# Seven products instead of eight for pairs 3 and 6 in the last projection's later blocks

## The chip, the core and the metric

The kernel runs on one core of a Trainium2 chip. Its engines, each with an instruction queue of its own that runs in order, are TensorE (PE, with the weight loads PEld), VectorE (DVE), ScalarE (ACT), GpSimd (POOL) and SyncE (SP). DMAs are issued here by SP and by POOL, a few by ACT, and 16 DMA engines move the data. The metric is the time of one execution on the device in microseconds (us); lower is better. Before the change the median of three runs is 2599.01 us (2597.99 to 2599.30).

## What is computed

Two layers of an encoder over 256 tokens of 4096 features. Each layer normalises, projects with one matrix to 11264 columns, mixes by grouped attention in one half of the features and by a retention in both directions in the other, and projects back with a 4096 x 4096 matrix:

```python
for l in range(DEPTH):                       # 2
    h = rmsnorm(x, norm_w[l])
    proj = h @ w_in[l]                       # 256 x 4096 @ 4096 x 11264
    ...
    x = x + jnp.concatenate([a_out, r_out], axis=-1) @ w_out[l]   # 4096 x 4096
return rmsnorm(x, final_norm)
```

All of it is float32. The change lies in the last product with `w_out` (the second layer's).

## The kernel before

**Stages and blocks.** The four projections are stages 0 to 3; stage 3 is the second layer's output projection. A stage is cut into blocks of 1024 output columns (two halves of 512), and stage 3 has four of them, b = 0 to 3. Within a block the 4096 rows of the weights are taken as 16 pairs of 128-row tiles, p = 0 to 15. A pair is a 2 x 2 block product: two halves of 128 tokens, two row tiles, two column halves, so eight products of 128 x 128 x 512, added up in eight banks M1 to M8 (in the profile all are called M).

**Eight or seven.** Some pairs are done with seven products instead, by a Strassen-like scheme: PE then multiplies sums of operand quarters by sums of weights, and the banks are combined at the block's end (`combine`; `last_combine` in the last block). `SEVENS` lists these pairs: 2, 5, 8, 9, 11 and 13 in every stage. Operands of a seven-product pair have seven forms: three quarters as they are (A11, A12, A22) and four sums (S1 to S4).

**Three matmuls a product.** PE takes float32r parts, so each operand and weight is split into a high part (a cast on ACT) and a low part (the difference, on DVE), and a product is high x high, high x low and low x high. `whi` and `wlo` are the two parts of a weight page, `x8h` and `x8l` those of an eight-product pair's operand, `x7h` and `x7l` those of a seven-product pair's. The first two matmuls are on L1683, the third on L1693. A page is 128 x 1024 numbers (512 KB) and serves several products.

**Weights of a pair.** An eight-product pair has two pages, loaded by SP into one of six buffers `wraw` and split. A seven-product pair loads one `wraw` page (kind A); ACT copies it to `wv`, POOL adds a prepared second tensor to that by an accumulating DMA (`twice_out`, kind T), SP loads half a page `third` (kind B, split into `bhi` and `blo`), and DVE forms `wu` from these three by two additions (kind U). The `twice` tensors are laid out on the host for the pairs of `EVER`, which are all pairs in `SEVENS`.

**What sets the order.** The program is recorded once in Python, and the order of every engine's queue is the order of recording. `block` walks over the products in the order of `GROUPS` (each group starts with a seven-product pair; eight-product pairs behind it are interleaved by `pages_of`); the class `Weights` keeps the pages ahead, with 5 buffers `whi` and 4 `wlo`. A planner with its own clocks for DVE and ACT (`tick`, `room`, `Lane`) slips in other work: output sums, `out_tasks`, operand splits. 13 buffers `pg` (`page`) hold everything else. In the last layer `out_task` loads a page `gain` by SP, and DVE multiplies the block's result by it (`ca<-ca,gain`, `cb<-cb,gain`).

**Operands.** `split_operand` and `split_pair` make a stage's operand parts from rows that `Turn` fetches from `next_dram`, two pairs at a time; the fetched page is dropped when both are split.

**The last block.** `last_combine` adds the residual, loaded by four DMAs of SP into the operand buffers of pairs 0 and 1 as soon as these are used up, and scales the output. The pairs in `DELAYED` (10, 12, 14, 15) leave their last products to the very end; parts of their weight pages are kept in operand buffers of pairs that are done (`dead_room`), so names such as `x7h` then hold weights.

Of the kernel before, what the change touches and what calls it, by code (L numbers as in the profile page):

```python
# [17 lines left out]
P = 128  # L18
# [144 lines left out]
def constants():  # L163
# [48 lines left out]
]  # L212

GROUPS = [
    ([tuple(range(_s[0]))] if _s[0] else []) + [tuple(range(_a, _b)) for _a, _b in zip(_s, _s[1:] + (NP,))] for _s in SEVENS
]
SPREAD = (3, 5, 8, 11, 12, 13)
SPREAD1 = (4, 7, 8, 10, 12, 14)
# [11 lines left out]
    return order  # L230


def grouped(order, stage):

    groups = []
    for p in order:
        if p in SEVENS[stage] or not groups:
# [6 lines left out]
FIRST_GROUPS = [grouped(_o, _i) for _i, _o in enumerate(FIRST_ORDER)]  # L244
# [4 lines left out]
def pages_of(group, stage, first=False):  # L249

    n = 1 if group[0] in SEVENS[stage] else 0
# [12 lines left out]

def slots_of(group, stage, first=False):

    for _p, _k in pages_of(group, stage, first):
        if _p in SEVENS[stage] and not (first and _p in NATIVE):
# [68 lines left out]
def hybrid_encoder(  # L337
# [451 lines left out]
    def split_pair(p, v, whole, stage):  # L789
# [748 lines left out]

    def lead(stage):

        return 8 * SEVENS[stage][0]

    def block(after_pair, phase, then, first_order=False, opening=False, order=LAST_ORDER, last=None, hurried=False):

# [42 lines left out]
        def begin_product(n, name, p, index, k, h):  # L1587
# [508 lines left out]
```

## Time and profile before

| | |
|---|---|
| median of 3 runs | 2599.01 us |
| the profiled execution | 2599.34 us |
| its span, first to last instruction | 2597.6 us |
| granted TensorE clock, mean | 0.998 |
| PE busy | 2581.8 us, 11560 matmuls |
| DVE, ACT, POOL busy | 2215.3, 1853.6, 398.6 us |
| moved by DMA | 653.52 MB, 252 GB/s in the mean |

The page gives each engine's busy time and its share of the span, then groups of equal instructions with their count, busy time, mean length, and the idle time of the engine just ahead of them with what ended it (after the arrow). A timeline row has its start and length in us, the engine, the line, the operation, what it writes and reads, and in brackets the idle time before it. In the table by windows an engine's busy time is followed by its number of instructions, and the last three columns are PE's granted clock, the mean busy share of the DMA engines and GB/s. Nearly all of DVE's and ACT's work is on L321, since a helper records it, so one goes by the names.

### The profile page before, as it was taken

To read this page: it belongs to the slowest core of one execution; us is meant where nothing else is said; L and a number is where in the kernel's file an instruction comes from. 1 tells how busy PE (TensorE), PEld (TensorE's weight loads), DVE (VectorE), ACT (ScalarE), POOL (GpSimd) and SP (SyncE) were. 2 spreads that over 40 slices of the span, in tenths; PEclk is the share of its full clock that TensorE was granted. 3 is DMA by queue.
4 is the path that set the end of the run, shared out by engine and by line. 5 is a ranking of instruction groups with operands and counts; after the bars stand their busy time and mean duration, and the time that the engine had idled before them with its cause. 6 is when DMAs were issued, how large, how long until landed. Compare 5 with 4: busy or idle time off the path is not lost.

```text
span 2597.6 us, 34368 instructions
## 1 busy us (share of the span) xinstructions
PE 2581.8 (99%) x11560; PEld 2135.2 (82%) x11560; DVE 2215.3 (85%) x2710; ACT 1853.6 (71%) x2626; POOL 398.6 (15%) x548
## 2 busy tenths in 40 slices
PE   9999999999999999999999999999999999999998
PEld 7888888888888888888878888888888888888886
DVE  7898888888789898777979888889888798987777
ACT  8877777766666788656887667776666667886655
POOL 0111221221102100211111112221201021000000
PEclk9999999999999999999999999999999999999999
DMA  9988988888778778988888879888887787788886
GB/s 314 305 237 277 289 242 254 281 247 263 221 220 260 230 235 227 271 269 248 275 253 261 250 239 279 246 270 268 259 257 222 208 259 242 220 229 251 250 243 194
DMA packets 206594, 653.52 MB, mean 252 GB/s; under 512 B 24784, under 2 KB 31440, under 8 KB 206416
## 3 DMA queue, kind: packets, MB, share of 16 engines
q1 hardware_dynamic: 147040, 472.99, 51.8%
q0 software_dynamic: 58656, 177.24, 30.7%
q8 instruction: 90, 1.47, 0.2%
q10 hardware_dynamic: 720, 1.10, 0.1%
q14 instruction: 88, 0.72, 0.1%
HBM read 607.19 MB, written 44.04 MB: 251 GB/s over the span
## 4 chain that ended last, share of the span: by engine, by line
PE 94%; DMA 2%; DVE 2%; ACT 1%; issue 1%; SPq 0%; DVEq 0%; POOLq 0%; POOL 0%; ACTq 0%
PE M L1683 60%; PE M L1693 30%; PE M L1158 1%; PE M L1157 1%; PE M L1156 1%; DMA ca<-in_x 1%; DVE wlo L321 1%; ACT whi L321 1%; DMA third<-in_w_out 0%; PE M L1677 0%; DMA wraw<-in_w_out 0%; DVE cb L321 0%; DMA whole<-in_w_in 0%; ACT ca L321 0%; DVE ca L321 0%
## 5 line engine op out<-in xcount | busy, mean ns | idle before, releaser
L321 DVE TENSOR_TENSOR wlo<-wraw,whi 128x1024 fp32r<-128x1024 f32 (+1 forms) x774 | 935.3, 1215 | 172.8 <-issue 61.2
L321 ACT CAST whi<-wraw 128x1024 fp32r<-128x1024 f32 (+1 forms) x776 | 800.1, 1045 | 297.1 <-PE M L1683 283.0
L1683 PE MATMUL M<-whi,x8h 128*128 128x512 f32 x2368 | 922.5, 390 | 1.0 <-DVE cb L321 0.8
L1683 PE MATMUL M<-whi,x8l 128*128 128x512 f32 x2368 | 921.8, 389 | 0.0
L1693 PE MATMUL M<-wlo,x8h 128*128 128x512 f32 x2364 | 676.3, 389 | 0.2 <-DVE wlo L321 0.2
L1683 PEld LDWEIGHTS M<-whi,x8h 128*128 128x128 f32 x2368 | 444.6, 188 | 94.9 <-DVE cb L321 1.5
L1683 PEld LDWEIGHTS M<-whi,x8l 128*128 128x128 f32 x2368 | 444.6, 188 | 92.4 <-DVE x8l L321 0.3
L1693 PEld LDWEIGHTS M<-wlo,x8h 128*128 128x128 f32 x2364 | 442.2, 188 | 91.4 <-DVE wlo L321 1.0
L1683 PE MATMUL M<-whi,x7h 128*128 128x512 f32 x1080 | 420.5, 389 | 0.2 <-ACT whi L321 0.2
L1683 PE MATMUL M<-whi,x7l 128*128 128x512 f32 x1080 | 420.3, 389 | 0.0
L1693 PE MATMUL M<-wlo,x7h 128*128 128x512 f32 x1080 | 334.4, 390 | 0.7 <-DVE wlo L321 0.6
L729 POOL DMA_DIRECT2D wv<-in_twice_in x132 | 118.5, 898 | 1068.6 <-ACT wv L321 923.8
L321 ACT CAST whi<-wu 128x1024 fp32r<-128x1024 f32 x180 | 189.3, 1052 | 91.9 <-DVE wu L321 54.2
L321 ACT CAST whi<-wv 128x1024 fp32r<-128x1024 f32 x180 | 189.0, 1050 | 91.5 <-PE M L1683 51.9
L321 DVE TENSOR_TENSOR wlo<-wv,whi 128x1024 fp32r<-128x1024 f32 x180 | 219.6, 1220 | 37.3 <-PE M L1693 30.7
L321 ACT COPY wv<-wraw 128x1024 f32<-128x1024 f32 x180 | 188.9, 1049 | 74.7 <-DMA wraw<-in_w_out 35.2
L321 DVE TENSOR_TENSOR wlo<-wu,whi 128x1024 fp32r<-128x1024 f32 x180 | 219.1, 1217 | 24.8 <-PE M L1693 16.7
L1693 PEld LDWEIGHTS M<-wlo,x7h 128*128 128x128 f32 x1080 | 202.4, 188 | 44.1 <-DVE wlo L321 2.5
L1683 PEld LDWEIGHTS M<-whi,x7h 128*128 128x128 f32 x1080 | 202.8, 188 | 42.6 <-ACT whi L321 0.9
L1683 PEld LDWEIGHTS M<-whi,x7l 128*128 128x128 f32 x1080 | 202.8, 188 | 41.8
L321 DVE TENSOR_TENSOR wu<-wu,third 128x512 f32<-128x512 f32 x180 | 124.6, 692 | 7.0 <-DMA third<-in_w_in 0.8
L321 DVE TENSOR_TENSOR wu<-wraw,wv 128x512 f32<-128x512 f32 x180 | 123.1, 684 | 8.7 <-DMA wv<-in_twice_in 6.3
(249 smaller groups left out, 2292.0 us busy)
## 6 DMA issues: line engine op xcount, KB each, us to landing
wraw<-in_w_in SPq DMA_DIRECT2D x568, 512.0 KB, 5.2
wraw<-in_w_out SPq DMA_DIRECT2D x208, 512.0 KB, 5.4
wv<-in_twice_in POOLq DMA_DIRECT2D x132, 512.0 KB, 7.5
third<-in_w_in SPq DMA_DIRECT2D x132, 256.0 KB, 5.8
wv<-in_twice_out POOLq DMA_DIRECT2D x48, 512.0 KB, 8.1
third<-in_w_out SPq DMA_DIRECT2D x48, 256.0 KB, 5.7
full<-next_dram POOLq DMA_DIRECT2D x18, 512.0 KB, 9.5
p_dram<-room POOLq DMA_DIRECT2D x64, 128.0 KB, 3.4
```

The costliest lines, as they stand in the source:

```text
L321: return call(out, *args, **kwargs)
L729: self.adds.pop(0)[1]()
L1156: nc.tensor.matmul(out, a[0], b[0], start=start, stop=False)
L1157: nc.tensor.matmul(out, a[0], b[1], start=False, stop=False)
L1158: nc.tensor.matmul(out, a[1], b[0], start=False, stop=stop)
L1683: nc.tensor.matmul(acc[name], a[i], g.hi[h], start=m == first[name] and not i, stop=False)
L1693: nc.tensor.matmul(acc[name], a, g.lo[h], start=False, stop=m == final[name])
```

## The change

Pairs 3 and 6 (`FLEX`) take seven products too in stage 3's blocks 1 and 2; in block 3, the last, pair 3 alone does. Block 0 stays as it was. In these blocks the pairs' order changes as well, so that sevens and other pairs alternate where they can: 0, 2, 1, 3, 4, 5, 6, 7, 8, 9, 10, 11, 13, 12, 14, 15 in blocks 1 and 2, and 0, 2, 1, 3, 4, 5, 6, 8, 7, 9, 10, 11, 13, 12, 14, 15 in the last.

Pairs 3 and 6 are split as eight-product pairs as before. Their three plain quarters are taken from `x8h` and `x8l`. For the four sums the rows are fetched a second time (`again`, a POOL DMA from `next_dram`) and a small task makes them and their two parts in one page `xs`, once each for the whole stage; two of the 13 `pg` pages stay taken by them.

```diff
+FLEX = (3, 6,)
+LATER = [tuple(sorted(_s + (FLEX if _i == 3 else ()))) for _i, _s in enumerate(SEVENS)]
 EVER = sorted(set(_p for _s in SEVENS for _p in _s))
+TWICE = sorted(EVER + list(FLEX))
...
+END_FLEX = (3,)
+END_SPREAD = (1, 3, 5, 7, 9, 11, 12)
+LATE_SPREAD = (1, 3, 5, 6, 8, 9, 11, 12)
+def late_order(sevens, spread):
+    order = [_p for _p in range(NP) if _p not in sevens]
+    for i, p in zip(spread or sevens, sevens):
+        order.insert(i, p)
+    return order
+GROUPS[3] = grouped(late_order(LATER[3], LATE_SPREAD), LATER[3])
+END_SEVENS = tuple(sorted(SEVENS[3] + END_FLEX))
+END_GROUPS = grouped(late_order(END_SEVENS, END_SPREAD or LATE_SPREAD), END_SEVENS)
+def plan_of(stage, b):
+    if not b:
+        return FIRST_GROUPS[stage], SEVENS[stage]
+    if stage == 3 and b == N_OUT2 - 1:
+        return END_GROUPS, END_SEVENS
+    return GROUPS[stage], LATER[stage]
...
+        if stage == 3 and p in FLEX:
+            tasks.append(Lane(more_forms(p), need=3, gate=forms_due))
         operand[p] = (hi, lo)
...
+    def forms_due():
+        return not waiting and not turning and not late
+    def more_forms(p):
...
+        v = fetch(next_dram[p // 2], "again")
+        yield FETCH
...
+        both = page([P, 2, 4, P], "xs", F32R)
+        f = page([P, 4, P], "xf")
+        s4, s1, s2, s3 = (tokens(f)[:, i] for i in range(4))
+        ve.tensor_sub(s1, x1[:, 1], x1[:, 0])
+        ve.scalar_tensor_tensor(s2, s1, -1.0, x0[:, 0], op0=ALU.mult, op1=ALU.subtract)
+        yield
+        ve.tensor_sub(s3, x0[:, 0], x1[:, 0])
+        ve.tensor_add(s4, x0[:, 1], s2)
+        yield
+        ac.copy(both[:, 0], f)
+        yield
+        ve.tensor_sub(both[:, 1], f, f32(both)[:, 0])
+        drop(2)
+        forms[p] = both, ve.until + PASS
...
+            elif p in sevens and p in FLEX:
+                while p not in forms:
+                    advance()
+                now.wait(forms[p][1])
+                if index[1] in (A11, A12, A22):
+                    i, m = {A11: (0, 0), A12: (1, 0), A22: (1, 1)}[index[1]]
+                    a = at(operand[p], ALL, i, slice(m * P, (m + 1) * P))
+                else:
+                    a = [forms[p][0][:, i, (S4, S1, S2, S3).index(index[1])] for i in range(2)]
```

The rest passes the list of sevens of a block, instead of the stage, to `grouped`, `pages_of`, `slots_of`, `Weights` and `block`, and lays out `twice` for the pairs of `TWICE`. Lines behind the new code move down: L321, L1683 and L1693 become L353, L1760 and L1770.

All queues are the same up to the last stage's block 0, PE's up to its block 1. Three places show what moves.

On PE, in block 1, the first page (kind A) of pair 3. Before, four products, 12 matmuls, on the parts `x8h` and `x8l`:

```order
L1683 MATMUL M_21134<-whi,x8h 128x512
L1683 MATMUL M_21134<-whi,x8l 128x512
L1683 MATMUL M_21141<-whi,x8h 128x512
L1683 MATMUL M_21141<-whi,x8l 128x512
L1683 MATMUL M_21154<-whi,x8h 128x512
L1683 MATMUL M_21154<-whi,x8l 128x512
L1683 MATMUL M_21157<-whi,x8h 128x512
L1683 MATMUL M_21157<-whi,x8l 128x512
L1693 MATMUL M_21134<-wlo,x8h 128x512
L1693 MATMUL M_21141<-wlo,x8h 128x512
L1693 MATMUL M_21154<-wlo,x8h 128x512
L1693 MATMUL M_21157<-wlo,x8h 128x512
```

Now two products, one on a plain quarter (`x8h`, `x8l`) and one on a sum (`xs`, which holds both parts):

```order
L1760 MATMUL M_21205<-whi,x8h 128x512
L1760 MATMUL M_21205<-whi,x8l 128x512
L1760 MATMUL M_21147<-whi,xs 128x512 x2
L1770 MATMUL M_21205<-wlo,x8h 128x512
L1770 MATMUL M_21147<-wlo,xs 128x512
```

The pair's four pages have 6, 6, 3 and 6 matmuls now, 21 in all, where two pages of 12 stood.

On SP, in the last block, around the four residual loads (from `x_dram`, into the buffers `x8l` and `x8h`). Before:

```order
L531 DMA wraw_22533<-in_w_out 128x1024
L552 DMA third<-in_w_out 128x512
L531 DMA wraw_22573<-in_w_out 128x1024
L2020 DMA x8l<-x_dram 128x512
L2020 DMA x8h<-x_dram 128x512
L2020 DMA x8l<-x_dram 128x512
L2020 DMA x8h<-x_dram 128x512
L1748 DMA gain<-in_final_norm 128x512
L531 DMA wraw_22596<-in_w_out 128x1024
```

Now:

```order
L585 DMA third<-in_w_out 128x512
L564 DMA wraw_22646<-in_w_out 128x1024
L564 DMA wraw_22652<-in_w_out 128x1024
L1825 DMA gain<-in_final_norm 128x512
L2097 DMA x8l<-x_dram 128x512
L2097 DMA x8h<-x_dram 128x512
L2097 DMA x8l<-x_dram 128x512
L2097 DMA x8h<-x_dram 128x512
L564 DMA wraw_22697<-in_w_out 128x1024
L585 DMA third<-in_w_out 128x512
```

The block's first `gain` has moved ahead of the residual loads; the second stands five weight loads behind them before and four now.

On DVE, the end of the last block's weights: the last low parts, up to the first sum of the banks (`cb<-ca,M`). `wlo<-wu` is the last page of pair 13, the last seven; the operations of 512 columns are half low parts of eight-product pairs, some into operand buffers. Before:

```order
L321 TENSOR_TENSOR wlo<-wv,whi 128x1024
L321 TENSOR_TENSOR blo<-third,bhi 128x512
L321 TENSOR_TENSOR x7l<-wraw_22929,whi 128x512
L321 TENSOR_TENSOR x7h<-wraw_22929,x7h 128x512
L321 TENSOR_TENSOR wlo<-wu,whi 128x1024
L321 TENSOR_TENSOR x7h<-wraw_22937,whi 128x512
L321 TENSOR_TENSOR x7l<-wraw_22937,x7l 128x512
L321 TENSOR_TENSOR cb<-ca,M_22699 128x512
```

Now:

```order
L353 TENSOR_TENSOR wlo<-wv,whi 128x1024
L353 TENSOR_TENSOR blo<-third,bhi 128x512
L353 TENSOR_TENSOR wlo<-wraw_22924,whi 128x512
L353 TENSOR_TENSOR x8l<-wraw_22924,x8h 128x512
L353 TENSOR_TENSOR wlo<-wu,whi 128x1024
L353 TENSOR_TENSOR wlo<-wraw_22965,whi 128x512
L353 TENSOR_TENSOR x7h<-wraw_22965,x8h 128x512
L353 TENSOR_TENSOR x7h<-wraw_22996,whi 128x512
L353 TENSOR_TENSOR x7l<-wraw_22996,x8l 128x512
L353 TENSOR_TENSOR x7h<-wraw_23054,whi 128x512
L353 TENSOR_TENSOR x7l<-wraw_23054,x7l 128x512
L353 TENSOR_TENSOR cb<-ca,M_22686 128x512
```

Behind `wlo<-wu` stood two half low parts, and now there are six.

More of the change, by code (lines that the diff above doesn't have):

```diff
@@ L214 @@
 GROUPS = [
-    ([tuple(range(_s[0]))] if _s[0] else []) + [tuple(range(_a, _b)) for _a, _b in zip(_s, _s[1:] + (NP,))] for _s in SEVENS
+    ([tuple(range(_s[0]))] if _s[0] else []) + [tuple(range(_a, _b)) for _a, _b in zip(_s, _s[1:] + (NP,))] for _s in LATER
 ]
@@ L230, in opening_order, with grouped @@
     return order
-def grouped(order, stage):
+def grouped(order, sevens):
     groups = []
     for p in order:
-        if p in SEVENS[stage] or not groups:
+        if p in sevens or not groups:
             groups.append(())
@@ L240, in grouped, with pages_of @@
     return groups
+END_FLEX = (3,)
[15 more added lines that the diff above has]
+    return GROUPS[stage], LATER[stage]
 FIRST_ORDER = [opening_order(_i) for _i in range(4)]
-FIRST_GROUPS = [grouped(_o, _i) for _i, _o in enumerate(FIRST_ORDER)]
+FIRST_GROUPS = [grouped(_o, SEVENS[_i]) for _i, _o in enumerate(FIRST_ORDER)]
 LEADS = [8 * next(_i for _i, _p in enumerate(_o) if _p in SEVENS[_s]) for _s, _o in enumerate(FIRST_ORDER)]
 SHARED = ("M1", "M5", "M7", "M6")
-def pages_of(group, stage, first=False):
-    n = 1 if group[0] in SEVENS[stage] else 0
+def pages_of(group, sevens, first=False):
+    n = 1 if group[0] in sevens else 0
     order, one, rest = [], group[:n], group[n:]
@@ L262, in pages_of, with slots_of @@
     return order + rest
-def slots_of(group, stage, first=False):
-    for _p, _k in pages_of(group, stage, first):
-        if _p in SEVENS[stage] and not (first and _p in NATIVE):
+def slots_of(group, sevens, first=False):
+    for _p, _k in pages_of(group, sevens, first):
+        if _p in sevens and not (first and _p in NATIVE):
             yield [(_b, _p, (ALL, _a), _k, _h) for _b, _a, _pg, _h in SEVEN_PRODUCTS if _pg == _k]
@@ L490, in __init__ @@
                         start = (l, b) == (0, 0) and w is w_in
-                        for g in GROUPS[stage] if b else FIRST_GROUPS[stage]:
-                            for slot in slots_of(g, stage, start):
+                        groups, sevens = plan_of(stage, b)
+                        for g in groups:
+                            for slot in slots_of(g, sevens, start):
                                 one = Page()
@@ L495, in __init__ @@
                                 one.whole = start and one.pair in NATIVE
-                                one.seven = one.pair in SEVENS[stage] and not one.whole
+                                one.seven = one.pair in sevens and not one.whole
                                 one.begun, one.low_at, one.empty, one.raw_at = False, None, False, 1e9
@@ L504, in __init__ @@
                                     if one.kind == PAGE_A:
-                                        self.sevens.append(Seven(w[l, b, one.pair], twice[l, b, EVER.index(one.pair)]))
+                                        self.sevens.append(Seven(w[l, b, one.pair], twice[l, b, TWICE.index(one.pair)]))
                                     one.own = self.sevens[-1]
@@ L851, in split_pair, with tokens @@
         yield
-    as_it_comes = {}
+    as_it_comes, forms = {}, {}
+    def forms_due():
+        return not waiting and not turning and not late
+    def more_forms(p):
+        def tokens(v):
+            return v.rearrange("p k (a t) -> p k a t", t=BLK)
+        v = fetch(next_dram[p // 2], "again")
+        yield FETCH
+        w = v.rearrange("p (a m i t) -> p m i a t", a=4, m=MT, t=BLK)[:, :, 2 * (p % 2) : 2 * (p % 2) + 2]
+        x0, x1 = w[:, 0], w[:, 1]
+        both = page([P, 2, 4, P], "xs", F32R)
[12 more added lines that the diff above has]
+        forms[p] = both, ve.until + PASS
+        own(-1)
+        pledge(0)
+        yield
     def split_operand(c, stage, rest=0.0):
@@ L1552, in block @@
         rush[0] = RUSH if hurried else 0.0
-        for g in FIRST_GROUPS[stage] if opening else GROUPS[stage]:
-            for slot in slots_of(g, stage, first_order):
+        groups, sevens = plan_of(stage, 0 if opening else N_OUT2 - 1 if last else 1)
+        for g in groups:
+            for slot in slots_of(g, sevens, first_order):
                 flat += slot
@@ L2061, in twice @@
     def twice(o):
-        d = np.empty(o.shape[:2] + (len(EVER), P, 2, NB), o.dtype)
-        for i, p in enumerate(EVER):
+        d = np.empty(o.shape[:2] + (len(TWICE), P, 2, NB), o.dtype)
+        for i, p in enumerate(TWICE):
             for h in range(2):
```

4 lines of the change are left out of this document (2 added, 2 removed).

## The prediction

> **What bounds the kernel now.** I read the page's busy shares and its chain first, then the waits of TensorE (PE), then the stretches of the last stage.
>
> ```profile
> span 2597.6 us, 34368 instructions
> PE 2581.8 (99%) x11560; PEld 2135.2 (82%) x11560; DVE 2215.3 (85%) x2710; ACT 1853.6 (71%) x2626; POOL 398.6 (15%) x548
> ...
> PE 94%; DMA 2%; DVE 2%; ACT 1%; issue 1%; SPq 0%; DVEq 0%; POOLq 0%; POOL 0%; ACTq 0%
> ```
>
> PE is busy for 99% of the span and carries 94% of the chain that ends last. The page alone would let an instruction taken from PE be worth its whole length; whether it is, the changed stretch must tell. That is the last stage's blocks 1 to 3, about 83 us each:
>
> ```profile
> core 0: us, PE busy (x) PEld busy (x) DVE busy (x) ACT busy (x) POOL busy (x), PEclk, DMA share, GB/s
> 2336.00:2419.00 83.00, 83.00 (x368) 68.76 (x367) 64.34 (x68) 51.79 (x61) 6.97 (x8) 1.00 0.82 239
> 2419.00:2502.00 83.00, 83.00 (x368) 68.75 (x367) 64.25 (x67) 51.92 (x60) 6.96 (x8) 1.00 0.81 241
> 2502.00:2586.00 84.00, 83.10 (x365) 68.00 (x363) 66.78 (x86) 49.87 (x71) 6.69 (x8) 1.00 0.75 222
> ```
>
> One row is one block. In blocks 1 and 2 PE never stops; VectorE (DVE) has 64.3 of 83 us, ScalarE (ACT) 52, the DMA engines 0.82. Everything but PE has room. The list of PE's waits over the whole stage (2240 to 2600 us) has a single row:
>
> ```profile
> PE M L1693 <- DVE wlo L321: 0.6, 1, 0.6
> ```
>
> The timeline shows where it is, in the last block:
>
> ```profile
> 2570.09 1.22 DVE L321 TENSOR_TENSOR wlo<-wu,whi 128x1024 fp32r<-128x1024 f32 x1
> ...
> 2571.36 0.50 PE L1693 MATMUL M<-wlo,x7h 128*128 128x512 f32 x1 [0.61 <-DVE wlo L321]
> ```
>
> So the stage is PE's, with a weak place near its end, where DVE delivers the low parts of weights just too late.
>
> **What goes.** A pair done with eight products takes 24 matmuls (three for each), one with seven takes 21. Blocks 1 and 2 change two pairs each, the last block one: 5 pairs, 15 matmuls. Their price is the pitch, not the 390 ns of one, since matmuls overlap:
>
> ```profile
> 2424.22 1.81 PE M L1683 x8
> ```
>
> 1.81 / 8 = 0.2266 us, and 15 x 0.2266 = **3.40 us**. PE was full around all of them, so this is on the path, as long as PE stays fed.
>
> **What is added, and what hides it.** By groups of block 1, DVE first, then ACT:
>
> ```profile
> L321 DVE TENSOR_TENSOR wlo<-wraw,whi 128x1024 fp32r<-128x1024 f32 x27 | 32.9, 1222 | 12.0 <-issue 5.5 <-PE M L1693 4.1 <-ACT whi L321 1.8
> L321 DVE TENSOR_TENSOR wlo<-wv,whi 128x1024 fp32r<-128x1024 f32 x6 | 7.3, 1224 | 1.9 <-PE M L1693 1.9
> L321 DVE TENSOR_TENSOR wlo<-wu,whi 128x1024 fp32r<-128x1024 f32 x6 | 7.3, 1224 | 2.3 <-PE M L1693 2.0
> L321 DVE TENSOR_TENSOR wu<-wu,third 128x512 f32<-128x512 f32 x6 | 4.2, 692 | 0.2
> L321 DVE TENSOR_TENSOR wu<-wraw,wv 128x512 f32<-128x512 f32 x6 | 4.1, 686 | 0.0
> L321 DVE TENSOR_TENSOR blo<-third,bhi 128x512 fp32r<-128x512 f32 x6 | 4.1, 684 | 0.0
> ...
> L321 ACT CAST whi<-wraw 128x1024 fp32r<-128x1024 f32 x28 | 29.2, 1054 | 21.6 <-PE M L1683 21.1 <-ACT whi L321 0.5
> L321 ACT CAST whi<-wv 128x1024 fp32r<-128x1024 f32 x6 | 6.3, 1053 | 3.1 <-PE M L1683 2.8 <-DMA wv<-in_twice_out 0.3
> L321 ACT CAST whi<-wu 128x1024 fp32r<-128x1024 f32 x6 | 6.3, 1052 | 4.2 <-DVE wu L321 1.9 <-PE M L1683 1.8 <-ACT bhi L321 0.5
> L321 ACT COPY wv<-wraw 128x1024 f32<-128x1024 f32 x6 | 6.3, 1051 | 4.0 <-DMA wraw<-in_w_out 3.5 <-DVE wlo L321 0.5
> L321 ACT CAST bhi<-third 128x512 fp32r<-128x512 f32 x6 | 3.7, 619 | 0.6 <-PE M L1683 0.6
> ```
>
> A pair that turns from eight to seven loses one subtraction `wlo<-wraw` on DVE and gains `wlo<-wv`, `wlo<-wu`, two `wu` and `blo`: 1.224 + 0.692 + 0.686 + 0.684 = +3.29 us. ACT loses one cast and gains three and a copy: 1.053 + 1.052 + 1.051 + 0.619 - 1.054 = +2.72 us. Two such pairs bring DVE in block 2 from 64.3 to 70.8 of 81.6 us and ACT from 51.9 to 57.4.
>
> The new forms of pairs 3 and 6 are made once each, one set in block 0, one early in block 1: four small DVE operations and a subtraction of 512 columns, a cast of 512 on ACT. The nearest rows are those that the old seven pairs use:
>
> ```profile
> 2275.61 0.29 DVE L321 TENSOR_TENSOR xf<-xf,full 128x128 f32<-128x128 f32 x1 [0.45 <-ACT xf L321]
> ```
>
> 4 x 0.29 + 0.68 = 1.8 us of DVE a set, so block 1 comes to 64.3 + 6.6 + 1.8 = 72.7 of 81.6 us. The covers are PE's matmuls of those blocks; I cost all this at nothing. The first row above shows the cover: DVE idled 12.0 us ahead of `wlo` in this block, much of it because PE had not yet given a buffer back, so DVE was ahead of PE. If this cover failed in full, 3.29 us a pair would reach PE, less that idle time.
>
> What an average does not show is the row of sevens: 5, 6, 8, 9 and 11 follow each other with only 7 and 10 between. That is five sevens and two eights, 153 matmuls, and PE needs 153 x 0.2266 = 34.7 us. DVE needs 1.222 + 2 x 1.224 + 0.692 + 0.686 + 0.684 = 5.73 us for a seven and 2.44 for an eight, 33.5 in all by full lengths. So over the worst run DVE still keeps pace, with 1.2 us to spare; the two `gain` products of 1.22 us that can fall into it leave it 1.3 us behind, which its lead at the start has to cover. I take 0, with 0 and +1.3 as ends.
>
> DMA: the same block's queues,
>
> ```profile
> q1 hardware_dynamic: 4896, 15.73, 53.9%
> q0 software_dynamic: 1123, 4.08, 27.6%
> ```
>
> give 53.9% x 83 / 15.73 = 2.84 us of all 16 engines per MB on SP's queue and 27.6% x 83 / 4.08 = 5.6 on POOL's. A changed pair drops one 0.52-MB page, adds a 0.26-MB `third` on SP and a 0.52-MB accumulating `wv` on POOL: -0.75 + 2.9 = +2.2 us, for two pairs 4.4 of 83, share 0.82 to 0.87. Each `again` fetch (0.52 MB, POOL) is once 2.9 us more. DVE's read of it stands in order ahead of low parts, which would wait with it. The nearest landings, from the page's list of DMA issues (the last number is us to landing):
>
> ```profile
> full<-next_dram POOLq DMA_DIRECT2D x18, 512.0 KB, 9.5
> ```
>
> and the slowest of POOL's in the last block:
>
> ```profile
> cb<-x_dram POOLq DMA_DIRECT2D x1, 512.0 KB, 10.9
> ```
>
> The code puts the read 13 us after the issue (FETCH) in its own count, later than 9.5 and than 10.9, so I take 0; a fetch as late again as the slower row is later than the median (1.4 us) still lands in time. POOL, which issues it and the added `wv`, is busy 7 of 83 us and nothing on it becomes late by two more.
>
> **The last block** is where cover is thin. Four waits tell why:
>
> ```profile
> 2516.53 1.05 ACT L321 COPY wv<-wraw 128x1024 f32<-128x1024 f32 x1 [6.44 <-DMA wraw<-in_w_out]
> 2517.48 2.00 ACT L321 CAST whi<-wraw 128x1024 fp32r<-128x1024 f32 x2
> ...
> 2521.30 0.39 PE L1683 MATMUL M<-whi,x8h 128*128 128x512 f32 x1
> ...
> 2526.88 1.23 DVE L321 TENSOR_TENSOR ca<-ca,gain 128x1024 f32<-128x1024 f32 x1 [3.69 <-DMA gain<-in_final_norm]
> 2529.34 1.22 DVE L321 TENSOR_TENSOR wlo<-wraw,whi 128x1024 fp32r<-128x1024 f32 x1
> ...
> 2531.27 0.39 PE L1693 MATMUL M<-wlo,x8h 128*128 128x512 f32 x1
> ...
> 2539.69 1.23 DVE L321 TENSOR_TENSOR cb<-cb,gain 128x1024 f32<-128x1024 f32 x1 [2.85 <-DMA gain<-in_final_norm]
> ```
>
> ACT waits 6.44 us for raw weights, and the page that it casts from 2517.48 (done about 2518.5) is used at 2521.30: a lead of 2.8 us. Then DVE stands 3.69 us behind `gain`, and the low part that ends at 2530.56 is used at 2531.27: 0.7 us. It stands again for 2.85 us, never catches up, and at 2571 PE waits. The change puts 3.29 us more on DVE here, but SP now issues the first `gain` ahead of the four residual rows instead of behind them, which should take away most of the 3.69 us; the second moves up by one weight load. Bounds: from -0.6 (the old wait goes) to +3.3 (all of the added work reaches PE). The nearest rows, 3.29 against 3.69, cancel, so I take **0**: the 0.6 us stay.
>
> The very end: the last sum of the seventh pair's group, `cb<-ca,M`, now has six half low parts of about 0.60 us behind the last `wlo<-wu` where there were two. After it DVE had this to spare before the last bank:
>
> ```profile
> 2585.75 0.69 DVE L321 TENSOR_TENSOR ca<-ca,M 128x512 f32<-128x512 f32 x1 [1.77 <-PE M L1693]
> ```
>
> 4 x 0.60 - 1.77 = +0.6 if DVE is as late as before, nothing if `wlo<-wu` comes earlier by what was moved behind it, which is what such a move does. I take 0.
>
> **Sum.** -3.40 + 0 + 0 + 0 = -3.4 us. The profiled execution took 2599.34 us (span 2597.6): it would take 2595.9. It stands 0.3 above the median of the three runs, 2599.01 (2597.99 to 2599.30); against that median the forecast is **2595.6**, 0.13% less. A measurement of this kernel can tell about 0.2%, 5.2 us: the forecast lies within it.
>
> **The rivals.** (B) The last block gives the saving back. DVE is full from 2539.69 to the end, so every us added behind that point reaches PE: 3.29 - 3.40 = -0.1 us at worst, 2598.9; with half of it, 2597.3. For it speaks the 0.7 us of lead; against it the place of `gain`.
>
> (C) It ends slower. In the last block the raw weights of pair 3, now a seven, come late by the same 6.44 us, while the residual rows and `gain` fill the queues. It decides once the lateness is above the lead that is left. With 0.7 us left, 5.7 us of PE time are lost: +2.3 us, 2601.3; twice that loss, 2607. Against it: SP issues the same number of pages in all, and PE has never waited for a raw page in this stage. [...]
>
> ```profile
> 2520.00:2560.00 40.00, 40.00 (x178) 33.15 (x177) 32.80 (x38) 30.23 (x43) 3.49 (x4) 1.00 0.95 270
> 2560.00:2600.00 40.00, 25.10 (x109) 19.96 (x108) 26.75 (x48) 14.28 (x26) 1.13 (x2) 0.87 0.37 137
> ```
>
> The granted clock is 1.00 with the 0.6-us wait near, and 0.87 only where PE is idle after 2585.7. [...]
>
> (D) More is won: DVE ends early, the 0.6 us go, and the end with its many small steps shortens by up to 1.8 us, the idle time of that last row. 2599.01 - 3.4 - 0.6 - 1.8 = 2593.2 at most. For it speaks nothing but that row.
>
> **Chances.** Forecast 0.60 (2594.5 to 2596.7: the old wait gone, or about one us of new ones); B 0.25 (to 2599.0); C 0.10; D 0.05. Forecast and B hold 0.85, so the range is 2594.5 to 2599.0, which takes in the ends of the DVE terms up to +3.3 one at a time. Faster by over 0.2% is under 2593.8: part of D, 0.03. Slower is over 2604.2: the far part of C, 0.03. The rest, 0.94, is within.
>
> **What would show it.** In the changed profile: 15 matmuls fewer; in blocks 1 and 2 windows of about 81.6 us with PE full and no PE wait, DVE near 71 to 73 and DMA near 0.87; the first `gain` wait of the last block short; the wait at `wlo<-wu` no longer than 0.6 us; the last bank's sum 0.4 us after the last matmul. PE waiting for `wlo` in the row of sevens, or for `whi` behind `wv`, would prove the zero of the added work wrong; a wait for raw weights in the last block would be C.

## The result, and the profile after

| | before | after |
|---|---|---|
| median, 16 runs each | 2599.02 us (2596.06 to 2601.22) | 2593.84 us (2592.64 to 2595.31) |
| profiled execution, its span | 2599.34, 2597.6 us | 2593.16, 2591.4 us |
| matmuls | 11560 | 11545 |

The ratio is 0.998, 95% interval [0.9973, 0.9987]: 5.2 us less, where 3.4 were forecast. The time is 0.7 us below the low end of the predicted range.

The page of the changed kernel: its span, the busy engines, and the engines' shares of the chain that ended last.

```profile
span 2591.4 us, 34411 instructions
...
PE 2577.2 (99%) x11545; PEld 2132.6 (82%) x11545; DVE 2233.3 (86%) x2740; ACT 1864.9 (72%) x2643; POOL 403.7 (16%) x555
...
PE 97%; DVE 1%; DMA 1%; ACT 1%; issue 0%; SPq 0%; POOLq 0%; POOL 0%; DVEq 0%; ACTq 0%
```

The table by windows of the changed kernel, one row for each of blocks 1 to 3:

```profile
core 0: us, PE busy (x) PEld busy (x) DVE busy (x) ACT busy (x) POOL busy (x), PEclk, DMA share, GB/s
2334.00:2415.60 81.60, 81.60 (x362) 67.57 (x361) 71.58 (x82) 55.54 (x66) 7.83 (x9) 1.00 0.89 254
2415.60:2497.20 81.60, 81.60 (x362) 67.57 (x361) 69.60 (x75) 56.00 (x67) 8.70 (x10) 1.00 0.89 252
2497.20:2581.20 84.00, 82.78 (x366) 68.21 (x364) 71.44 (x91) 52.71 (x75) 7.53 (x9) 1.00 0.75 225
```

Blocks 1 and 2 take 81.6 us with PE full, against 83.0 before; DVE has gained 5 to 7 us and DMA 0.07 to 0.08. The list of PE's waits between 2240 and 2600 us, which had one row before, is empty.

The timeline of the changed kernel at the places of the last block that the prediction spoke of:

```profile
2511.42 0.46 SPq L1825 DMA_DIRECT2D gain<-in_final_norm  x1
...
2523.42 1.23 DVE L353 TENSOR_TENSOR ca<-ca,gain 128x1024 f32<-128x1024 f32 x1 [1.10 <-ACT gain L353]
...
2534.44 1.23 DVE L353 TENSOR_TENSOR cb<-cb,gain 128x1024 f32<-128x1024 f32 x1 [1.10 <-ACT gain L353]
...
2561.50 1.22 DVE L353 TENSOR_TENSOR wlo<-wu,whi 128x1024 fp32r<-128x1024 f32 x1
...
2565.77 0.62 PE L1770 MATMUL M<-wlo,x7h 128*128 128x512 f32 x2
```

DVE no longer waits for the DMA of `gain` (what is left, 1.10 us, is the wait for ACT, which first writes its squares into a half of that page), and the last `wlo<-wu` ends at 2562.72, 3.05 us ahead of its use; before it ended 0.05 us ahead of PE, which stood there.

**Where the 5 us came from.** I cut each trace by its matmuls. *Gaps* are, for one block, the distances between the starts of following matmuls, summed, less 0.2267 us each. The *end* is the time from the start of the last matmul to the end of the span.

- Matmuls: 15 x 0.2267 = 3.40 us.
- Gaps of the last block: 1.01 us before, 0.00 after. Blocks 1 and 2 have none in either.
- End: 12.24 before, 11.76 after, 0.48 less.

That is 4.89 of the 5.18 us between the medians; the 0.29 left over is within the interval, 3.6 us wide. The two profiled executions lie further apart (6.2 us of span), since block 1 starts 1.3 us earlier in the one of after, behind code that is the same in both; in the profiles of the twelve runs below this start lies between 2333.7 and 2337.9 us, without a system.

### The profile page after: what moved, and what is told of

It reads as the page before. It is cut to its first block, busy times and chain, and to the rows that moved or that the text cites. A ratio compares the mean times of both kernels' runs of the same rounds, so it can differ in the third digit from the quotient of the medians.

```text
span 2591.4 us, 34411 instructions
## 1 busy us (share of the span) xinstructions
PE 2577.2 (99%) x11545; PEld 2132.6 (82%) x11545; DVE 2233.3 (86%) x2740; ACT 1864.9 (72%) x2643; POOL 403.7 (16%) x555
## 4 chain that ended last, share of the span: by engine, by line
PE 97%; DVE 1%; DMA 1%; ACT 1%; issue 0%; SPq 0%; POOLq 0%; POOL 0%; DVEq 0%; ACTq 0%
PE M L1760 62%; PE M L1770 31%; PE M L1225 1%; PE M L1224 1%; PE M L1223 1%; DMA ca<-in_x 0%; PE M L1754 0%; DVE cb L353 0%; DVE wlo L353 0%; ACT ca L353 0%; DVE ca L353 0%; DMA whole<-in_w_in 0%; ACT whi L353 0%; ACT wv L353 0%; DVE x7h L353 0%
## 5 line engine op out<-in xcount | busy, mean ns | idle before, releaser
L353 DVE TENSOR_TENSOR wlo<-wraw,whi 128x1024 fp32r<-128x1024 f32 (+1 forms) x769 | 929.8, 1215 | 159.3 <-PE M L1770 52.8
L353 ACT CAST whi<-wraw 128x1024 fp32r<-128x1024 f32 (+1 forms) x771 | 795.8, 1045 | 279.1 <-PE M L1760 263.2
L1760 PE MATMUL M<-whi,x8h 128*128 128x512 f32 x2338 | 910.8, 390 | 0.5 <-DVE ca L353 0.3
L1760 PE MATMUL M<-whi,x8l 128*128 128x512 f32 x2338 | 910.0, 389 | 0.0
L1770 PE MATMUL M<-wlo,x8h 128*128 128x512 f32 x2334 | 669.4, 389 | 0.0
L1760 PEld LDWEIGHTS M<-whi,x8h 128*128 128x128 f32 x2338 | 439.0, 188 | 93.1 <-DVE ca L353 1.0
L1760 PEld LDWEIGHTS M<-whi,x8l 128*128 128x128 f32 x2338 | 439.0, 188 | 91.0 <-issue 0.2
L1770 PEld LDWEIGHTS M<-wlo,x8h 128*128 128x128 f32 x2334 | 436.5, 188 | 89.9 <-DVE wlo L353 0.7
L1760 PE MATMUL M<-whi,x7h 128*128 128x512 f32 x1080 | 420.5, 389 | 0.2 <-ACT whi L353 0.2
L1760 PE MATMUL M<-whi,x7l 128*128 128x512 f32 x1080 | 420.3, 389 | 0.0
L1770 PE MATMUL M<-wlo,x7h 128*128 128x512 f32 x1080 | 334.2, 389 | 0.2
L353 ACT CAST whi<-wu 128x1024 fp32r<-128x1024 f32 x185 | 194.6, 1052 | 98.2 <-DVE wu L353 61.5
L353 ACT CAST whi<-wv 128x1024 fp32r<-128x1024 f32 x185 | 194.2, 1050 | 87.5 <-PE M L1760 50.7
L353 DVE TENSOR_TENSOR wlo<-wv,whi 128x1024 fp32r<-128x1024 f32 x185 | 225.7, 1220 | 34.1 <-PE M L1770 26.9
L353 ACT COPY wv<-wraw 128x1024 f32<-128x1024 f32 x185 | 194.2, 1050 | 74.5 <-DMA wraw<-in_w_out 32.2
L353 DVE TENSOR_TENSOR wlo<-wu,whi 128x1024 fp32r<-128x1024 f32 x185 | 225.3, 1218 | 20.6 <-PE M L1770 13.7
L1770 PEld LDWEIGHTS M<-wlo,x7h 128*128 128x128 f32 x1080 | 202.6, 188 | 42.9 <-DVE wlo L353 1.0
L1760 PEld LDWEIGHTS M<-whi,x7h 128*128 128x128 f32 x1080 | 202.8, 188 | 42.4 <-ACT whi L353 0.8
L1760 PEld LDWEIGHTS M<-whi,x7l 128*128 128x128 f32 x1080 | 202.8, 188 | 41.7
L353 DVE TENSOR_TENSOR wu<-wraw,wv 128x512 f32<-128x512 f32 x185 | 126.6, 685 | 10.6 <-DMA wv<-in_twice_in 8.4
L353 DVE TENSOR_TENSOR wu<-wu,third 128x512 f32<-128x512 f32 x185 | 128.0, 692 | 6.4
```

Source lines behind the costliest of these rows:

```text
L353: return call(out, *args, **kwargs)
L1760: nc.tensor.matmul(acc[name], a[i], g.hi[h], start=m == first[name] and not i, stop=False)
L1770: nc.tensor.matmul(acc[name], a, g.lo[h], start=False, stop=m == final[name])
```

## The experiments

This table has the terms for every run, in us: matmuls fewer x 0.2267, the gaps of blocks 1, 2 and 3, the end, what these make against before (gaps 1.01, end 12.24), and beside it the measured difference of the medians. The terms come from one execution, the medians from 11 runs of each kernel beside 33 of before (16 and 16 for the change; 10 for e4_natural, whose run of 3849.78 us is left out).

| run | fewer | gaps 1, 2, 3 | end | by terms | by medians | ratio's interval |
|---|---|---|---|---|---|---|
| the change | 15 | 0, 0, 0 | 11.76 | -4.89 | -5.18 | 0.9973 to 0.9987 |
| e1_middle | 12 | 0, 0, 0.88 | 11.75 | -3.34 | -2.86 | 0.9982 to 0.9999 |
| e3_order | 0 | 0, 0, 0 | 12.23 | -1.02 | -0.94 | 0.9989 to 1.0006 |
| e5_gain | 0 | 0, 0, 0.45 | 12.22 | -0.58 | -0.36 | 0.9989 to 1.0006 |
| e6_late4 | 15 | 0, 0, 0 | 11.76 | -4.89 | -4.85 | 0.9974 to 0.9992 |
| e2_last | 3 | 0, 0, 0.88 | 11.86 | -1.19 | -1.39 | 0.9987 to 1.0005 |
| e4_natural | 15 | 0, 6.61, 2.46 | 11.75 | +4.17 | +2.86 | 1.0002 to 1.0020 |
| e9_before_sp8 | 0 | 0, 0, 1.41 | 12.38 | +0.54 | -0.67 | 0.9987 to 1.0005 |
| e10_after_sp8 | 15 | 0, 0, 0 | 12.13 | -4.52 | -4.76 | 0.9972 to 0.9990 |
| e11_midnat | 15 | 3.37, 5.58, 1.04 | 11.75 | +5.09 | +1.44 | 1.0000 to 1.0018 |
| e12_endnat | 15 | 0, 0, 3.47 | 11.76 | -1.42 | -0.21 | 0.9987 to 1.0005 |
| e14_three | 21 | 4.92, 0.68, 0 | 11.74 | -0.67 | -0.15 | 0.9990 to 1.0008 |
| e7_end6 | 18 | 0, 0, 1.83 | 11.75 | -3.75 | -3.15 | 0.9978 to 0.9996 |

An interval is 0.14 to 0.18% wide, 3.6 to 4.7 us: single medians don't resolve one us. The terms do, as far as one execution goes: where there are no gaps in a block, there are none to 0.01 us.

### Blocks 1 and 2 alone: e1_middle

```diff
-END_FLEX = (3,)
+END_FLEX = ()
-END_GROUPS = grouped(late_order(END_SEVENS, END_SPREAD or LATE_SPREAD), END_SEVENS)
+END_GROUPS = grouped(range(NP), END_SEVENS)
```

> Changed kernel, but its last block as before: natural order, six sevens, so 12 matmuls fewer instead of 15. If blocks 1 and 2 give only their matmuls, -12 x 0.2266 = -2.72 us against before (about 2596.3), the first gain wait of the last block (3.7 us of DVE), PE's wait for wlo<-wu (0.6 us) and the 12.2 us from the last matmul to the end all stand as before. If instead the blocks in the middle brought the part beyond the 3.4 us (spread order, other DMA timing), -4 us or more and the last block unchanged.

The two blocks give their 2.72 us and nothing more, and the last block has its wait again; the list of PE's waits of this run, 2240 to 2597 us (engine, line, what it waited for: us in total, times, longest):

```profile
PE M L1770 <- DVE wlo L353: 0.6, 1, 0.6
```

Against the expectation the end is short all the same, 11.75: that term belongs to neither the last block's order nor its pair.

### The last block's order alone: e3_order

```diff
-FLEX = (3, 6,)
+FLEX = ()
-END_FLEX = (3,)
-LATE_SPREAD = (1, 3, 5, 6, 8, 9, 11, 12)
+END_FLEX = ()
+LATE_SPREAD = None
-END_GROUPS = grouped(late_order(END_SEVENS, END_SPREAD or LATE_SPREAD), END_SEVENS)
+END_GROUPS = grouped([0, 2, 1, 3, 4, 5, 6, 8, 7, 9, 10, 11, 13, 12, 14, 15], END_SEVENS)
```

> No pair changes its number of products: blocks 1 and 2 as before, only the last block's order is that of the change (0 2 1 3 4 5 6 8 7 9 10 11 13 12 14 15), with pair 3 an eight. Matmuls as before, 11560. Theory A, the order of the last block frees DVE (no wait for gain, the weights' low parts ahead of PE): the 0.6 to 1.0 us of PE's wait go and the tail behind the last matmul shortens by about 0.5, so -1.1 to -1.5 us. Theory B, only the number of matmuls counts and the rest of the measured 5.2 us is scatter: 0, within 0.3 us.

With not one matmul fewer, the 1.01 us of gaps go. The end stays at 12.23. The median moves by -0.94, as the terms say, though its interval holds zero.

### The early gain alone, and the late gain in the change: e5_gain, e6_late4

In before, both loads are issued at the start of the task, and nothing else differs:

```diff
-    def out_task(l, n, res):
+    def out_task(l, n, res, fn=None):
...
-            fn = load_gain(n)
+            fn = fn or load_gain(n)
...
     def out_tasks(l, n, c):
...
+        fns = [load_gain(2 * n + i) if (l, n) == (DEPTH - 1, N_OUT2 - 2) else None for i in range(2)]
         second = now.t + LANDING
         yield max(0.0, LANDING - APART)
-        one = out_task(l, 2 * n, c[0])
+        one = out_task(l, 2 * n, c[0], fns[0])
...
-            yield from out_task(l, 2 * n + 1, c[1])
+            yield from out_task(l, 2 * n + 1, c[1], fns[1])
```

> Before, with nothing changed but that SP issues the two gain loads of the last block some 10 us earlier, ahead of the four residual rows; DVE's order is that of before, instruction by instruction. Theory A1, late gain was what made DVE late: the waits of 3.69 and 2.85 us go, DVE stays 2 us or more ahead at the last wlo<-wu, PE's 0.6 us go, and perhaps the 0.5 us of the tail: -0.6 to -1.5 us. Theory A2, it was the row of neighbouring sevens: DVE's time before gain is used up behind ACT's and PE's own pace, PE's wait stays at 0.5 us or more, and the time within 0.3 us of before.

In the change, the first of them is issued later:

```diff
         if last:
+            d = 4.0 if n == N_OUT - 4 else 0.0
+            if d:
+                yield d
             fn = load_gain(n)
             outs[n] = res
             own(-1)
-            yield LANDING
+            yield LANDING - d
```

> The changed kernel with one load moved: SP issues the first gain of the last block behind the four residual rows, as before the change did; all orders of DVE, ACT and PE are those of the change. Theory A1 (gain is the cause): DVE stands 2 to 4 us at ca<-gain, its smallest lead over PE (0.89 us) goes under 0, PE waits 0.6 to 2 us, the time is 0.5 to 2 us above the change. Theory A2 (the order alone is enough): DVE makes the wait good before the next weights are due, no PE wait, within 0.3 us of the change.

The timeline of e5_gain:

```profile
2505.47 2.61 SPq L1748 DMA_DIRECT2D gain<-in_final_norm  x2
...
2524.04 1.23 DVE L321 TENSOR_TENSOR ca<-ca,gain 128x1024 f32<-128x1024 f32 x1 [0.54 <-ACT gain L321]
...
2539.12 1.23 DVE L321 TENSOR_TENSOR cb<-cb,gain 128x1024 f32<-128x1024 f32 x1 [1.49 <-ACT gain L321]
...
2569.33 1.22 DVE L321 TENSOR_TENSOR wlo<-wu,whi 128x1024 fp32r<-128x1024 f32 x1
2570.61 0.30 PEld L1693 LDWEIGHTS M<-wlo,x7h 128*128 128x128 f32 x2 [0.57 <-DVE wlo L321]
```

and that of e6_late4, at the same product:

```profile
2526.88 1.23 DVE L353 TENSOR_TENSOR ca<-ca,gain 128x1024 f32<-128x1024 f32 x1 [2.74 <-DMA gain<-in_final_norm]
```

With `gain` in time DVE's waits for that load go, 6.54 us (3.69 + 2.85); waits of 0.54 and 1.49 us for ACT are left in their place. And yet `wlo<-wu` at 2569.33 starts only 0.76 us earlier than before (0.2 of it already there where block 1 starts) and is again just too late: the gaps are 0.45 us, where the profiles with the old last block and the late load have 1.01 (before), 0.88 (e1_middle) and 1.41 (e9_before_sp8). With the first `gain` late in the change, DVE stands 2.74 us, and PE doesn't notice. So the early load can be worth about half of the gap, but the order alone closes it, with the load early (e3_order) or late. Why shows in the waits of DVE and ACT over the last block, before first, then e5_gain, then e3_order:

```profile
DVE wlo L321 <- ACT whi L321: 5.1, 2, 4.6
...
ACT wv L321 <- DMA wraw<-in_w_out: 8.5, 3, 6.4
```

```profile
DVE wlo L321 <- ACT whi L321: 7.9, 3, 5.1
...
ACT wv L321 <- DMA wraw<-in_w_out: 10.5, 3, 6.9
```

```profile
DVE wlo L353 <- ACT whi L353: 1.7, 3, 1.2
...
ACT wv L353 <- DMA wraw<-in_w_out: 6.5, 3, 3.9
```

Much of what DVE wins at `gain` it loses at the next `whi` (7.9 us in place of 5.1): ACT is the late one, standing at a copy `wv<-wraw` for raw weights with casts behind it. In the new order ACT's longest such wait is 3.9 us instead of 6.4 and 6.9, and DVE waits 1.7 us for ACT instead of 5.1 and 7.9. The longest wait tells more than the sum: e6_late4, without a gap, has 3.8 us as its longest and 11.1 in all.

### The last block alone: e2_last

```diff
-FLEX = (3, 6,)
-LATE_SPREAD = (1, 3, 5, 6, 8, 9, 11, 12)
+FLEX = (3,)
+LATE_SPREAD = None
...
-    return GROUPS[stage], LATER[stage]
+    return (grouped(range(NP), SEVENS[stage]) if stage == 3 else GROUPS[stage]), SEVENS[stage]
```

> Only the last block is changed (order and pair 3 a seven: 3 matmuls fewer); blocks 1 and 2 as before. Theory A, matmuls plus the gaps that the new order closes: -0.68 for the matmuls and -1.01 for the gaps ahead of wlo<-wu in the last block, so -1.7 us, its matmuls without a gap. Theory B, the added 3.3 us of DVE work in the last block costs something once it is alone: less than -1.2. The end behind the last matmul is 12.2 us if SP runs as many instructions as before, 11.8 if some five fewer.

Theory A's price was wrong here: the old gap is gone, but another, 0.93 us from start to start, stands at the `blo` of pair 11. The same page is the one with the smallest lead in the other runs with this order: 1.09 us in e3_order (pair 3 an eight), 0.89 in the change, 0.50 in e6_late4. The last block's added pair fits with under 1 us to spare, and not in every execution of every schedule around it.

### The change with the pairs in the order 0 to 15: e4_natural, e11_midnat, e12_endnat

```diff
-END_SPREAD = (1, 3, 5, 7, 9, 11, 12)
-LATE_SPREAD = (1, 3, 5, 6, 8, 9, 11, 12)
+END_SPREAD = None
+LATE_SPREAD = None
```

> The change without the alternation: pairs 3 and 6 are sevens as in the change, but all three blocks keep the pairs in the order 0 to 15, so sevens stand side by side (2 3, 5 6, 8 9). Matmuls as in the change, 15 fewer. Theory A, in blocks 1 and 2 the order doesn't matter (DVE at 71 of 81.6 us, in lead), in the last block it does: the gap before wlo<-wu comes back at 1 us or more, since 3.3 us of DVE work are added and the gain load is late again: 1 to 3 us above the change, 2 to 4 us below before. Theory B, the alternation is what makes the added sevens free: gaps in blocks 1 and 2 too, 3 us or more above the change, the saving gone. Theory C, order is without meaning: as the change, within 0.3.

The list of PE's waits of e4_natural over the last stage, then what SP's queue waited for between 2420 and 2455 us, in block 2:

```profile
PE M L1760 <- ACT bhi L353: 2.8, 1, 2.8
PE M L1760 <- ACT whi L353: 0.8, 1, 0.8
PE M L1770 <- DVE wlo L353: 0.6, 1, 0.6
PE M L1770 <- DVE blo L353: 0.3, 1, 0.3
```

```profile
SPq L585 <- DVE blo L353: 12.3, 3, 10.1
SPq L564 <- DVE wu L353: 10.7, 4, 4.5
```

and the timeline of that place:

```profile
2442.02 0.69 DVE L353 TENSOR_TENSOR wu<-wu,third 128x512 f32<-128x512 f32 x1
2442.05 0.33 SPq L564 DMA_DIRECT2D wraw<-in_w_out  x1
...
2447.51 1.05 ACT L353 COPY wv<-wraw 128x1024 f32<-128x1024 f32 x1 [3.80 <-DMA wraw<-in_w_out]
...
2450.35 0.61 ACT L353 CAST bhi<-third 128x512 fp32r<-128x512 f32 x1
...
2451.02 0.80 PE L1760 MATMUL M<-bhi,x7h 128*128 128x512 f32 x1 [2.79 <-ACT bhi L353]
...
2454.42 0.63 PE L1760 MATMUL M<-whi,x7l 128*128 128x512 f32 x1
```

The chain that these rows show is a loop through four engines. A seven's raw page stays in one of the six `wraw` buffers until `wu` is formed, and `wu` needs the accumulating DMA of POOL (8.1 us to landing in the median of this run's page); only then does SP load the next raw page (2442.05, once `wu` has read the old one); ACT waits 3.80 us for that page at a copy, and the `bhi` that PE needs is queued behind the copy and two casts. SP in turn stood 10.1 us at a `third`, whose buffer comes free by `blo`, behind `bhi`. That the loop's own pace is the limit is read from this chain; no run changed a buffer. All the while DVE's sum is no larger than in the change: 69.5 us in this block, 69.6 there.

Which part of the order does it is open. In blocks 1 and 2 the two orders differ only in that the change has 2 ahead of 1 and 13 ahead of 12. Sevens stand side by side in both: 2 3, 5 6 and 8 9 here, and 5 6, 8 9 and 11 13 in the change, which has no gap. So "alternate where they can" says too much for these blocks, and neighbours alone are not the cause. The wait is at pair 5's page B, behind 2, 3, 4 in a row, where the change has 1 between 2 and 3; e11_midnat waits at the same matmul of its block 2.

Then there is the clock. As its 2.79 us of idling ended, PE fell to half its pace, 0.427 us from start to start, and stayed there for 6.8 us, until 2457.8. Windows of the same run:

```profile
2450.00:2455.00 5.00, 3.67 (x8) 2.47 (x9) 4.96 (x7) 4.32 (x6) 0.00 (x0) 0.60 0.92 197
2455.00:2460.00 5.00, 5.00 (x18) 3.95 (x17) 4.05 (x4) 3.13 (x3) 0.86 (x1) 0.72 0.85 280
2460.00:2465.00 5.00, 5.00 (x24) 4.14 (x23) 3.66 (x4) 2.33 (x3) 0.00 (x0) 1.00 1.04 224
```

The granted clock is 0.60, 0.72, and 1.00 again. Of the 6.61 us of gaps the wait is 2.95 (3.18 between two starts, less 0.23), the slow stretch 3.66, with a second wait of 0.31 us in it. One of the 11 runs of this kernel took 3849.78 us, at a granted clock of 0.63 in the mean; the others 2598.35 to 2605.77. What happened in it isn't known.

The two parts were then undone one at a time.

```diff
-GROUPS[3] = grouped(late_order(LATER[3], LATE_SPREAD), LATER[3])
+GROUPS[3] = grouped(range(NP), LATER[3])
```

> The change with only blocks 1 and 2 in the order 0 to 15; the last block keeps the change's order. In the run with all three blocks in that order block 2 lost 6.6 us: ACT stood 3.8 us at a copy wv<-wraw for raw weights, PE then 2.8 us at bhi, and after that wait PE ran some 6.8 us at half its pitch. Theory A, neighbouring sevens make ACT and DMA late, not DVE: block 2 again loses 3 to 7 us (with or without the slow stretch), the last block nothing; the time is 2597 to 2601. Theory B, the loss came from the last block's order (its loads come early into block 2): no gap in blocks 1 and 2, time as the change.

```diff
-END_GROUPS = grouped(late_order(END_SEVENS, END_SPREAD or LATE_SPREAD), END_SEVENS)
+END_GROUPS = grouped(range(NP), END_SEVENS)
```

> The change with only the last block in the order 0 to 15, pair 3 a seven in it. Theory A: blocks 1 and 2 as in the change without a gap, the last block loses 1.0 (the gap of before) to 2.5 us (as when all blocks had this order), so 2595 to 2596.5. Theory B, the last block's order is without meaning: as the change, 2593.9.

PE's waits in the last stage, e11_midnat first, then e12_endnat:

```profile
PE M L1760 <- ACT bhi L353: 2.6, 1, 2.6
PE M L1770 <- DVE blo L353: 2.5, 4, 0.8
```

```profile
PE M L1760 <- ACT whi L353: 2.3, 1, 2.3
```

Theory A holds in the main: each part loses its saving by itself. Its sizes don't: in e11_midnat block 1 lost 3.37 us too (none in e4_natural) and the last block, where nothing was expected, 1.04, and the profiled execution, 2604.01 us, is the slowest of its 11. In e12_endnat it is the third fastest (2596.01; median 2598.60), so most executions may lose more than its 3.47 us. These orders scatter from run to run, over 5.3 to 7.4 us, where the change's 16 runs lie within 2.7.

### More of the same: e14_three, e7_end6

```diff
-FLEX = (3, 6,)
+FLEX = (3, 6, 7)
-LATE_SPREAD = (1, 3, 5, 6, 8, 9, 11, 12)
+LATE_SPREAD = (1, 3, 4, 6, 7, 9, 10, 12, 13)
...
             if last_layer and final:
+                held[0] -= len(FLEX) - len(END_FLEX)
```

> More of the same: in blocks 1 and 2 pair 7 takes seven products too (three added pairs; order with nine sevens spread, 1 3 4 6 7 9 10 12 13), and the pages of its and pair 6's forms are given back ahead of the last block; 6 matmuls fewer than the change. If the work is still hidden, -1.36 us against the change (2592.5). DVE then has 72 + 3.3 = 76 of 80.9 us and DMA about 0.93. If the cover ends here, as raw weights come late to ACT's copies with nine sevens in a block, PE waits of 0.5 to 3 us in blocks 1 and 2, and the time is that of the change or above.

```diff
-END_FLEX = (3,)
-END_SPREAD = (1, 3, 5, 7, 9, 11, 12)
+END_FLEX = (3, 6)
+END_SPREAD = (1, 3, 5, 6, 8, 9, 11, 12)
```

> The change with pair 6 a seven in the last block too (order spread as in blocks 1 and 2): 3 matmuls fewer, -0.68 us. The smallest lead of DVE over PE in the change's last block is 0.9 us, at a blo of 0.69; 3.3 us more of DVE work there use it up if they come ahead of that place. Theory A: a gap of 0.5 to 2.5 us in the last block, time equal to the change or up to 1.5 above. Theory B, leads recover within a pair: -0.68, no gap, 2593.2.

PE's waits, e14_three first, then e7_end6:

```profile
PE M L1770 <- DVE blo L353: 2.3, 2, 1.9
PE M L1760 <- ACT bhi L353: 0.9, 1, 0.9
```

```profile
PE M L1770 <- DVE blo L353: 0.6, 1, 0.6
PE M L1760 <- ACT bhi L353: 0.3, 1, 0.3
```

Both lose more than they save: the third pair 5.60 us of gaps for 1.36 of matmuls (half-pace matmuls among them), pair 6 in the last block 1.83 for 0.68. The cover ends just behind what the change uses. No version of these is faster than the change.

### The end: e9_before_sp8, e10_after_sp8

Behind the last matmul all kernels but one (e9_before_sp8, below) do the same up to the last landing, 10.5 us later. The trace's own list of SP's closing instructions (us from the start of the last matmul) shows the difference, before first, then after:

```
before  ... semaphore 10.91-10.94   drain 11.27-11.40   drain 11.46-11.47 ...   end 12.24
after   ... semaphore 10.87-10.90   drain 10.94-10.94   drain 10.99-11.00 ...   end 11.76
```

In before SP stops for 0.33 us between its last semaphore waits and the first drain, without a wait that the trace shows; that drain then takes 0.13 us in place of less than 0.01. Before has 1876 instructions on SP, the change 1871, five semaphore waits fewer and as many loads. To move the place of the stop against these waits, eight tiny loads were added to SP's queue in each kernel:

```diff
         outs = {}
+        if last_layer:
+            tiny = t(cp, [1, 128], "tiny")
+            for i in range(8):
+                nc.sync.dma_start(tiny[:, 16 * i : 16 * i + 16], consts[:1, 16 * i : 16 * i + 16])
```

> Before, with eight tiny loads (64 bytes each, into a tile that nothing reads) issued by SP at the start of the last stage: eight instructions more on SP, nothing else. [...] Eight instructions more put it ahead of the first of these waits, where SP stands anyway: the end is 11.8, the time 0.5 us less than before. Rival, the 0.5 us have another cause: end 12.2, time as before or above.

> The change with the same eight tiny loads on SP. [...]

| SP instructions | kernels | where SP stops, us from the last matmul |
|---|---|---|
| 1885 | e9_before_sp8 | 6.12 to 6.47, nine instructions earlier than in before |
| 1880 | e10_after_sp8 | 10.69 to 11.02, four earlier |
| 1876 | before, e3_order, e5_gain | 10.94 to 11.27 |
| 1873 | e2_last | 11.16 to 11.52, three later |
| 1871 to 1869 | the change and the seven others | nowhere |

The stop keeps its place in SP's program: it stands ahead of the 1872nd of SP's instructions in each of the six kernels that have that many. And it is one of a row. In all 14 traces SP stands for 0.33 to 0.35 us ahead of its 720th instruction and of every 128th from there to the 1744th; where it waits for nothing elsewhere, it needs less than 0.07 us. The next place is the 1872nd, and the change ends with its 1871st. So the 0.48 us are an accident of how many semaphore waits the schedule leaves on SP. In e10_after_sp8, for which an end of 12.2 was expected and a time 0.5 us above the change, the stop comes back behind the last landing, and the end is 12.13 us, 0.37 more than in the change. In e9_before_sp8 the stop is hidden as expected, but against the expectation the end isn't shorter (12.38): the last landing came at 11.12 instead of 10.51, for a reason that one profile doesn't tell.

## Why the prediction was right or wrong

**Right: the matmuls.** 3.40 us by the pitch, with 81.60 for 82.96 us in each of blocks 1 and 2, and no gap there to eat it.

**Right in its result, with the wrong reason: the added work is hidden.** DVE came to 71.6 and 69.6 us (72.7 and 70.8 forecast), DMA to 0.89 (0.87). But I argued from DVE's sum over the row of sevens, 33.5 against 34.7 us, and took the order for no part of it. The row was also cut short: in the new order 13 stands right behind 11, and with it the same lengths make 39.3 against 39.4 us, next to nothing to spare. And of DVE's 12.0 us of idle time, of which I ascribed much to PE, the row puts 4.1 down to it. e4_natural has the same sums and lost all of the saving and more. By its trace what limits is the loop of raw buffers, ACT's copy and POOL's accumulating DMA, and the new order is what keeps the cost at nothing (no gaps in blocks 1 and 2 of the change, 8.95 us in e11_midnat). Rival C's mechanism, raw weights late to ACT, was the real danger (3.80 us in block 2 of e4_natural); I placed it in the last block only and didn't see that the order decides it.

**Wrong: the last block, "I take 0: the 0.6 us stay".** This is one of the two steps that put the time under the range. I had DVE standing behind `gain`, with 3.29 us of added work against 3.69 of wait. The runs show that `gain` is not what decides: without its wait 0.45 us of gaps are left (e5_gain), and with the first one late in the new order none (e6_late4). The late one was ACT, and the order of the pairs cures that (e3_order: 0, with no pair changed). The order stood in the change to be read; I priced pairs and loads and took the order for a detail. That the 3.29 us of added work cost nothing here is partly luck: the smallest lead left was 0.89 us, and e2_last, with the same last block, lost 0.88 us.

It was mis-sized as well. The row of waits counts from the modelled end of the matmul ahead, 0.39 us behind its start, while the next would start 0.23 behind it. So a "0.61" was 1.00 between starts, 0.77 us lost, and with the slower starts beside it 1.01.

**Wrong: the very end, 0.** The part I looked at was right: `wlo<-wu` now starts 18.1 us ahead of the last matmul in place of 15.2, more than the 2.4 us moved behind it, and DVE still idles ahead of the last bank, 1.99 us where it was 1.77:

```profile
2580.02 0.69 DVE L353 TENSOR_TENSOR ca<-ca,M 128x512 f32<-128x512 f32 x1 [1.99 <-PE M L1770]
```

The 0.48 us came from SP's stop, in a place where I had read no row.

With both terms the sum is 2599.01 - 3.40 - 1.01 - 0.48 = 2594.1, and 2593.84 was measured. Either term alone would have left the time in the range. Rival D had this side, at 0.05: I gave it "nothing but that row" to speak for it. Its 0.6 us did go, but that row's idle time did not shrink, so the shorter end that it forecast came for another reason. Rival B fell, since nothing was given back.

**The clock.** Rival C counted a loss of PE time at its length alone. In e4_natural PE ran at half its pace, 0.427 us from start to start, after 2.79 us of idling. In e11_midnat 2.62 us alone did not bring it, but a second wait of 0.80 us, 0.7 us later, did; in e14_three idle times of 0.85 and 1.94 us, 0.7 us apart, were enough, while a single 2.26 us in e12_endnat was not. So a wait can cost more than its length: the half pace lasted 3.4 us in e11_midnat and e14_three and 6.8 us in e4_natural, where it cost 3.7 us on a wait of 2.95. What decides whether it comes, and for how long, these four runs don't show.

## What to carry to other kernels

An engine's idle sum doesn't tell by itself whether added work is hidden: with the same sum on DVE, 69.5 and 69.6 us in block 2, e4_natural had 6.61 us of gaps there and the change none. The chain from a buffer's release to the next load and back is to be looked at beside the sums. Where a change brings a new order, the order is priced by itself, as a wait near the end may go with it (1.01 us of gaps in e3_order). A wait that is short in the list costs the distance between two starts less the pitch (0.77 us for a "0.61" here), and the last instructions of every queue, SP's too, belong to the end (0.48 us here).

## What the hardware showed

- Half pace after short idling: 2.79 us of an idle PE were followed by 6.8 us at 0.43 us a matmul (e4_natural; the granted clock was 0.60 and 0.72 in the two windows of 5 us that hold them, which makes 0.50 for the 6.8 us); two idle times 0.7 us apart, of 2.62 and 0.80 us (e11_midnat) or 0.85 and 1.94 us (e14_three), by 3.4 us of it.
- SP stops for 0.33 to 0.36 us ahead of every 128th instruction of its program, from the 720th to the 1744th in all 14 traces and the 1872nd in the six that have it; at the end of before nothing hid it (12.24 us from the last matmul, 11.76 in the change). What SP does in a stop the traces don't show: the one packet of 8192 bytes of the queue called instruction near the end of before starts 0.6 us behind the stop, not in it.
- An accumulating DMA of 512 KB took 8.1 us to land in the median (`wv<-in_twice_out`, the list of DMA issues on the pages of before, the change and e4_natural), and a raw buffer of a seven is held over it. More buffers (a third for `third`, a seventh for `wraw`) were not tried.
